# Values of the dilated head groups: which order of tokens the products read, and who regroups them

## The chip, the cores and the metric

The program runs on 1 core of one Trainium2 chip. The metric is the device time of one execution in microseconds (us), from the runs' own clock. The core has a matrix engine (TensorE: PE for the products, PEld for the loads of their stationary operand, the weights of a matmul), VectorE (DVE), ScalarE (ACT), GpSimd (POOL), and SyncE (SP), which only issues DMAs here. Each engine works through its own instructions in the order in which they are written. Two memories lie on the core: SBUF, 128 partitions wide, and PSUM, into which TensorE writes.

## The reference

A stack of transformer blocks over 512 tokens with a width of 1024, in float32. The change lies in the first two layers, whose mixer A is a dilated sliding-window attention in three groups of four heads. Group 0 reads neighbouring tokens; for group 1 (dilation 4) and group 2 (dilation 16) the tokens are regrouped first, so that every fourth (or sixteenth) token comes together:

```python
DSW_GROUPS = ((128, 1), (512, 4), (2048, 16))

def to_sub(a):
    a = a.reshape(B, L, dilation, H, hd).transpose(0, 2, 3, 1, 4)
    return jnp.pad(a, ((0, 0), (0, 0), (0, 0), (0, Lp - L), (0, 0)))
...
h = rmsnorm(x, norm1[l])
proj = h @ w_in[l]
qa, ka, va, qb, kb, vb, gate_pre = jnp.split(proj, splits, axis=-1)
...
p = jnp.exp(scores - mx)
den = jnp.sum(p, axis=-1, keepdims=True)
o = jnp.einsum('brhnqk,brhnkc->brhnqc', p, vw) / den
```

The values `va` of one group are 512 tokens by 256 columns (4 heads of 64). A second mixer B (`qb`, `kb`, `vb`), gates, an output product and a feed-forward part follow; further blocks after the second layer are not touched.

## The kernel before

**Products.** Every float32 operand is held as two float32r parts, `hi` and `lo`. `mm3` (L215 to L219) makes one product from three matmuls: hi*hi (L217), hi*lo (L218), lo*hi (L219). The weights of the model come as chunks of up to 1024 rows by 256 columns. `unit` (L495) takes 128 columns of a chunk as the stationary operand and streams the 512 tokens of x past them, 24 matmuls of 512 columns. `unit_tok` (L503) does it the other way: the stationary operand is 128 tokens of x (`xh[k][:, toks]`, a 128x128 block), and the chunk's 256 columns are streamed, again 24 matmuls (8 pieces of the width, three each). The result has tokens on partitions. One such unit of 128 tokens is called a tile here.

**Values.** `v_chunk` (L569) makes the values of one group in four tiles. With `perm`, which holds for `v1` and `v2`, tile j takes the tokens j, j+4, j+8, ...: `dsl(j, P, 4)` picks every fourth column of `xh` and `xl`, so that the regrouping happens in the read of the stationary operand. `vb` and `v0` take 128 neighbouring tokens, `slice(j * P, (j + 1) * P)`. ACT then moves the tile out of PSUM, scaled by the norm's factor of each token (L580), into `va[g]`, where each pair of heads has a block of ones between its two blocks of 64. The factors in regrouped order are columns 4 to 7 of `rcol`, made by four small DMAs from POOL in `norm_gen` (L473).

**Order.** Nothing is scheduled by a planner; the order of the Python code is the order on each engine. After each unit `tick` (L192) emits: pieces of the split of the next chunk (`pump`, L125: hi by ACT at L111, lo by DVE at L112) and, where a chunk is through, the load of the chunk three further on (L89, on SP's queue); then the evacuation of the unit; then one step of every background generator. The generators around the change are `mixer_b` (L652), whose last step is eight matmuls at L724 after the first tile of `v1`; `mixer_a_exp` (L761), which regroups the scores' maxima by DMAs from POOL (L770, L778) and then subtracts (DVE, L786) and takes exp (ACT, L787), one job a tick; and `mixer_a` (L795), which begins with the chunks `ga` after `v2`: transposes of the scores (L834), copies of them (L837), and, a tick later, the products with the values `va` (L819), in the order group 1, 2, 0.

**Buffers.** Tiles of 128x512 made by `t` (L62) share 45 buffers, those of PSUM share 8, raw chunks have 3. A new user of a buffer waits until the former one's last reader is done.

Of the kernel before, what the change touches and what calls it, by code (L numbers as in the profile page):

```python
# [4 lines left out]
F32 = mybir.dt.float32  # L5
# [6 lines left out]
P = 128  # L12
# [7 lines left out]
# columns of the packed parameters, each vector as columns of 128  # L20
# [11 lines left out]
# columns of the packed constants  # L32
# [8 lines left out]
class Ctx:  # L41
    """Pools, the weight stream and the clock that interleaves background work with dense units."""
# [82 lines left out]
    def pump(self, npieces=None):  # L125
        """Emit pieces of the split of the chunk after the one in use, and the loads behind it.

        Without a number: so many that the split is through a unit before the chunk in use is."""
        if npieces is None:
            left, self.ticks = self.ticks, max(1, self.ticks - 1)  # L130
            if not self.todo and self.nsplit < min(len(self.chunks), self.cur + self.ahead):
                self._start_split()
            npieces = -(-len(self.todo) // max(1, left - 1))
        self._pieces(npieces)
        while self.loaded < min(len(self.chunks), self.nsplit - (1 if self.todo else 0) + 3):
            self._load()
# [15 lines left out]
    def next(self, name, ticks=2):  # L152
        """(hi, lo) of the next chunk of the plan."""
        i = self.cur
        assert self.chunks[i]["name"] == name, (self.chunks[i]["name"], name)
        self.hl.pop(i - 2, None)
        self.ahead = 1
        while self.nsplit <= i or (self.nsplit == i + 1 and self.todo):
            self.pump(1)
        self.cur = i + 1  # L160
        self.ticks = ticks
        return self.hl.pop(i)

# [38 lines left out]
    def settle(self):  # L202
        """Emit what was put off to the next tick."""
        later, self.later = self.later, []
        for f in later:
            f()
# [14 lines left out]
    def split(self, src, name, scale=None):  # L221
        """hi and lo parts of src (times a column of scales)."""
        nc = self.nc
        h = self.t(name + "h", F32R)
        l = self.t(name + "l", F32R)
        n = src.shape[-1]
        hv, lv = h[:, 0:n], l[:, 0:n]
        if scale is None:
            nc.scalar.activation(hv, src, AF.Copy)
            nc.vector.tensor_tensor(lv, src, hv.bitcast(F32), op=SUB)  # L230
        else:
            nc.scalar.activation(hv, src, AF.Copy, scale=scale)
            nc.vector.scalar_tensor_tensor(lv, src, scale, hv.bitcast(F32), op0=MUL, op1=SUB)
        return hv, lv


class Parts:
    """Rows k, 256 columns each, two to a tile."""
# [24 lines left out]
def make_plan(a):  # L263
# [15 lines left out]
    # the first chunk comes in parts, to start early  # L279
# [51 lines left out]
    # the last products go through twice  # L331
# [19 lines left out]
class Kern(Ctx):  # L351
# [45 lines left out]
    def norm_begin(self, gain, gain2=None):  # L397
        """gain: fn(j) -> column of x's factor. gain2: fn(j), factor whose squares are also summed."""
        self.norm_ready = False
        self.ngain, self.ngain2 = gain, gain2  # L400
        self.xh, self.xl = [None] * KT, [None] * KT
        self.sqs = [[], []]

    def sumsq(self, src, slot, scale=None, apart=False, to=0, dve=False):
        """Add src's squares to one of the slot's list of sums, or start another."""
        nc = self.nc
        n = src.shape[-1]
        acc = self.sqs[slot]
        q = self.t("sq")[:, 0:n]
        if scale is None:  # L410
            nc.scalar.activation(q, src, AF.Square)  # L411
        else:
            nc.scalar.activation(q, src, AF.Square, scale=scale)
        if not acc or apart:
            acc.append(q)
        else:
            (nc.vector if dve else nc.gpsimd).tensor_tensor(acc[to], acc[to], q, op=ADD)  # L417

    def norm_tile(self, j):
        """Split of x[j] for the next products, and its squares."""  # L420
        g = self.ngain(j)
        self.xh[j], self.xl[j] = self.split(self.x[j], "x", scale=g)
        dve = j == KT - 1
        self.sumsq(self.x[j], 0, dve=dve)
        if self.ngain2 is not None:
            self.sumsq(self.x[j], 1, scale=self.ngain2(j), dve=dve)

    def rsqrt(self, v, n, out=None):
        """v^-0.5 of an SBUF tile [P, n]."""
        nc = self.nc  # L430
# [12 lines left out]
    def colsum(self, sq, nt, dim):  # L443
        """[P, nt] of mean + eps of the summed squares, tokens on partitions."""
# [11 lines left out]
    def rows(self, r, nt):  # L456
        """PSUM [P, nt*P]: r's columns as rows, the same on every partition."""
        ps = self.ps()
        for T in range(nt):
            self.nc.tensor.matmul(ps[:, T * P:(T + 1) * P], lhsT=r[:, T:T + 1].to_broadcast([P, P]), rhs=self.ident, start=True, stop=True)  # L460
        return ps[:, 0:nt * P]

    def norm_gen(self, perm=False, rows=True):
# [4 lines left out]
        rcol = self.pc.tile([P, 8], F32, tag="rcol", bufs=2, name=self.nm("rcol"))  # L468
        r = self.rsqrt(v, 4, None if two else rcol[:, 0:4])
        if perm:  # L470
            # every fourth token
            for T in range(4):
                nc.gpsimd.dma_start(rcol[32 * T:32 * T + 32, 4:8], rcol[:, T:T + 1])  # L473
        yield
        if two:
# [3 lines left out]
            # u = mean((x g)^2) + eps; wanted: r^2 mean + eps  # L479
# [15 lines left out]
    def unit(self, ps, hl, nt, ks, first=True, last=True, xs=None, k0=0):  # L495
        """Features nt*128.. of a chunk, transposed: out [features, tokens]."""
# [6 lines left out]
    def unit_tok(self, ps, hl, toks, xs=None, rhs=None):  # L503
        """Tokens of a chunk's all columns: out [tokens, columns]."""
# [8 lines left out]
    def late_pair(self, hl, early, late, xs=None, mid=None):  # L513
        """Two units at once: the operands of the late k come last."""
# [12 lines left out]
    def first_pair(self, hl, ev, gen):  # L527
        """The first two units after a norm: the last tiles of x come late."""
        p = self.late_pair(hl, range(0, 6), (6, 7), mid=gen)
        self.tick(lambda: ev(0, p[0]), lambda: ev(1, p[1]))  # L530
# [14 lines left out]
    def mixer1(self, l):  # L545
        nc = self.nc
        # per two heads: values, ones, values
# [21 lines left out]
        def v_chunk(name, dst, perm):  # L569
            hl = self.next(name, 4)  # L570
            for j in range(4):
                p = self.ps()
                self.unit_tok(p[:, 0:256], hl, dsl(j, P, 4) if perm else slice(j * P, (j + 1) * P))

                def ev(p=p, j=j):
                    o, i = dst[:, j], p[:, 0:256]
                    if dst is not vb:
                        o, i = o[:, :, dsl(0, 2, 2)], i.rearrange("p (a b c) -> p a b c", a=2, b=2)
                    c = 4 + j if perm else j
                    nc.scalar.activation(o, i, AF.Copy, scale=self.rcol[:, c:c + 1])  # L580
                self.tick(ev)

        if l == 0:
            # x comes in tile by tile
# [3 lines left out]
            self.first_pair(self.next("kb"), ev_q(kT, "b", None, False), self.norm_gen(perm=True))  # L588
        else:
            self.first_pair(self.next("qb"), ev_q(qT, "b", 0.125, False), self.norm_gen(perm=True))  # L590
# [22 lines left out]
        def ev_g(dst):  # L613
            # sigmoid(y) = (1 + tanh(y / 2)) / 2; kept: tanh
# [37 lines left out]
    def mixer_b(self, qT, kT, vb, oB):  # L652
# [3 lines left out]
        for hp in range(2):  # L656
            po = None
            for hh in range(2):
# [30 lines left out]
                # wide parts go in two passes  # L689
# [38 lines left out]
    def mixer_a_scores(self, g, qT, kT, st):  # L728
# [3 lines left out]
        # heads of one bank share their rows of the PE array  # L732
# [28 lines left out]
    def mixer_a_exp(self, st):  # L761
        """exp of the scores less the maximum over all groups."""
        nc = self.nc
        m = st["m"]
        # the maximum, in both orders of the tokens
# [145 lines left out]
    def mem_norm(self):  # L911
        """mem's mean squares: rows and columns of the factors."""
# [40 lines left out]
    def mem_k(self):  # L953
        """K^T [head dim, 256 tokens] of each head of the memory."""
# [10 lines left out]
    def mem_v(self, done=None):  # L965
        """V [tokens, heads * dim] of the memory."""
# [12 lines left out]
    def even(self):  # L979
# [50 lines left out]
        for i in range(2):  # L1030
# [26 lines left out]
            if i == 0:  # L1057
                # the norm between the blocks scales x itself
# [11 lines left out]
    def out_proj(self, name, cat, ks=range(8), late=2):  # L1070
        """x += the transposed product of the tiles cat with the next chunks; the last of ks come late."""
# [17 lines left out]
    def xattn(self, l):  # L1089
# [8 lines left out]
        def halves(v):  # L1098
            """The two parts of 256 columns in one tile."""
# [6 lines left out]
        def scores(h):  # L1106
            # softmax(r s): the queries' factors r are not yet in s
# [85 lines left out]
    def rope_table(self):  # L1193
        """Rows 64-95 cos, 96-127 the signed sin of the positions' angles, 0-63 ones."""
# [12 lines left out]
        # 2 pi in parts of few bits  # L1207
# [4 lines left out]
        # rows of cos: sin(pi/2 - |r|)  # L1212
# [10 lines left out]
    def odd(self):  # L1223
# [68 lines left out]
        # up-projections of the latents  # L1292
# [33 lines left out]
        # the matrix memory  # L1326
# [4 lines left out]
        # 2 sigmoid(y) = 1 + tanh(y / 2)  # L1331
# [34 lines left out]
        # the last heads come beside the first products  # L1366
# [46 lines left out]
    def mla(self, qT, kT, mv, ha):  # L1413
        nc = self.nc
        # queries' tile T: keys 0..(T+1)*128
# [76 lines left out]
    def mlstm_gates(self, gt, out):  # L1492
# [33 lines left out]
        # beside twice the sums  # L1526
# [11 lines left out]
    def mlstm(self, qm, km, vm, g4, so, hm, nv):  # L1538
# [24 lines left out]
        def s2(h):  # L1563
# [21 lines left out]
            # the last two heads' means side by side  # L1585
# [40 lines left out]
    def down_final(self, ah, al):  # L1626
        """The last products and the last norm, in halves of the tokens."""
# [176 lines left out]
```

## Time and profile before

| | |
|---|---|
| median of 3 runs | 2814.88 us (2813.25 to 2814.93) |
| profiled execution, span from first to last instruction | 2811.2 us |
| median less that span | 3.7 us |
| PE busy, DVE, ACT, POOL (share of the span) | 99%, 53%, 37%, 12% |
| mean granted TensorE clock | 0.996 |

The profile is of one execution, and its span leaves out what lies around the first and the last instruction; no time of its own beside the span is given for it, so the span and the median of the runs stand 3.7 us apart for whatever reasons. Busy shares are means over the whole span. Matmuls overlap: a row's duration is longer than the distance from its start to the next one's, and the distance is what a tile costs.

### The profile page before, as it was taken

How to read it: one execution, taken by the hardware profiler on the slowest of the kernel's cores; microseconds unless marked ns; L12 is line 12 of the kernel's file. 1: busy time of each engine (PE TensorE's matmuls, PEld its weight loads, DVE VectorE, ACT ScalarE, POOL GpSimd, SP SyncE). 2: the span in 40 equal slices, each digit the busy share in tenths (PEclk: the TensorE clock that was granted, in tenths of full speed). 3: DMA queues.
4: the chain of work that ended last, by engine and by line, in shares of the span. 5: the costliest groups of instructions: out<-in, count | busy, mean ns of one | idle time of the engine just before them, and what ended most of it. 6: DMA issues, size and time to landing. Idle time of an engine off the chain costs nothing.

```text
span 2811.2 us, 33273 instructions
## 1 busy us (share of the span) xinstructions
PE 2780.3 (99%) x13358; PEld 2320.8 (83%) x13358; DVE 1483.8 (53%) x2533; ACT 1046.7 (37%) x1967; POOL 340.2 (12%) x402
## 2 busy tenths in 40 slices
PE   9999999999999999999999999999999999999998
PEld 7798888888878988788888887888888788788887
DVE  5533765445554356645466666434356646643434
ACT  5333343333343434423243354322243535532223
POOL 2110110001111002201021111000011001110002
PEclk9999999999999999999999999999999999999999
DMA  5112323322321114223223323232232112333321
GB/s 186 60 48 66 98 90 105 102 94 79 109 82 46 60 61 135 90 90 104 92 89 109 105 83 116 91 104 90 94 88 86 46 54 82 105 97 98 100 88 53
DMA packets 245306, 251.42 MB, mean 89 GB/s; under 512 B 7424, under 2 KB 243200, under 8 KB 244640
## 3 DMA queue, kind: packets, MB, share of 16 engines
q1 hardware_dynamic: 242592, 243.58, 27.0%
q0 software_dynamic: 1552, 4.93, 0.5%
q8 instruction: 104, 1.70, 0.3%
q10 hardware_dynamic: 1008, 0.80, 0.1%
q14 instruction: 50, 0.41, 0.1%
HBM read 247.15 MB, written 2.10 MB: 89 GB/s over the span
## 4 chain that ended last, share of the span: by engine, by line
PE 93%; DVE 3%; ACT 2%; issue 1%; POOL 0%; DMA 0%; POOLq 0%; ACTq 0%; DVEq 0%
PE ps L217 29%; PE ps L218 28%; PE ps L219 28%; DVE lo L112 1%; PE ps L819 1%; PE ps L747 1%; PE ps L1476 1%; PE ps L724 1%; PE ps L667 1%; PE ps L1427 1%; DVE x L540 0%; PE ps L1151 0%; PE ps L834 0%; PE ps L451 0%; PE ps L460 0%
## 5 line engine op out<-in xcount | busy, mean ns | idle before, releaser
L217 PE MATMUL ps<-xh,hi 128*128 128x512 f32 x2224 | 875.1, 393 | 5.1 <-ACT hi L111 5.1
L219 PE MATMUL ps<-xh,lo 128*128 128x512 f32 x2224 | 868.9, 391 | 1.4 <-DVE lo L112 1.4
L218 PE MATMUL ps<-xl,hi 128*128 128x512 f32 x2224 | 868.5, 391 | 0.0
L112 DVE TENSOR_TENSOR lo<-raw,hi 128x512 fp32r<-128x512 f32 (+2 forms) x922 | 636.1, 747 | 197.2 <-ACT hi L111 196.0
L111 ACT ACTIVATE hi<-raw 128x512 fp32r<-128x512 f32 (+2 forms) x922 | 506.6, 617 | 324.7 <-PE ps L218 255.2
L217 PEld LDWEIGHTS ps<-xh,hi 128*128 128x128 f32 x2224 | 419.0, 188 | 93.4 <-ACT hi L111 5.7
L219 PEld LDWEIGHTS ps<-xh,lo 128*128 128x128 f32 x2224 | 418.9, 188 | 91.0 <-DVE lo L112 3.1
L218 PEld LDWEIGHTS ps<-xl,hi 128*128 128x128 f32 x2224 | 419.0, 188 | 84.9 <-issue 0.2
L218 PE MATMUL ps<-actl,hi 128*128 128x512 f32 (+1 forms) x752 | 282.7, 376 | 0.3 <-DVE actl L230 0.3
L217 PE MATMUL ps<-acth,hi 128*128 128x512 f32 (+1 forms) x752 | 282.8, 376 | 0.0
L219 PE MATMUL ps<-acth,lo 128*128 128x512 f32 (+1 forms) x752 | 282.6, 376 | 0.0
L540 DVE TENSOR_TENSOR x<-ps,x 128x512 f32<-128x512 f32 x136 | 93.5, 688 | 266.6 <-PE ps L219 266.6
L218 PEld LDWEIGHTS ps<-actl,hi 128*128 128x128 f32 x752 | 141.6, 188 | 26.0 <-DVE actl L230 0.5
L219 PEld LDWEIGHTS ps<-acth,lo 128*128 128x128 f32 x752 | 141.6, 188 | 25.6
L217 PEld LDWEIGHTS ps<-acth,hi 128*128 128x128 f32 x752 | 141.6, 188 | 25.5
L861 DVE TENSOR_TENSOR a<-ps,Rb 128x512 f32<-128x512 f32 x88 | 60.6, 691 | 182.4 <-PE ps L219 174.8
L417 POOL TENSOR_TENSOR sq<-sq,sq 128x512 f32<-128x512 f32 (+1 forms) x73 | 94.6, 1300 | 436.4 <-ACT sq L411 431.2
L872 POOL TENSOR_TENSOR y<-y,Rb 128x512 f32<-128x512 f32 x44 | 57.3, 1302 | 589.3 <-ACT y L868 589.3
L217 PE MATMUL ps<-hi,xh 128*128 128x256 f32 x384 | 128.3, 334 | 0.0
L872 POOL TENSOR_TENSOR a<-a,Rb 128x512 f32<-128x512 f32 x44 | 58.2, 1326 | 571.0 <-ACT a L871 571.0
L218 PE MATMUL ps<-lo,xh 128*128 128x256 f32 x384 | 123.4, 321 | 0.0
L219 PE MATMUL ps<-hi,xl 128*128 128x256 f32 x384 | 123.4, 321 | 0.0
(367 smaller groups left out, 3178.0 us busy)
## 6 DMA issues: line engine op xcount, KB each, us to landing
raw<-in_w_up SPq DMA_DIRECT2D x44, 1024.0 KB, 5.1
raw<-in_ffn_w_gate_up SPq DMA_DIRECT2D x44, 1024.0 KB, 5.1
raw<-in_w_in SPq DMA_DIRECT2D x39, 1024.0 KB, 5.1
raw<-in_w_down SPq DMA_DIRECT2D x16, 1024.0 KB, 5.1
raw<-in_ffn_w_down SPq DMA_DIRECT2D x16, 1024.0 KB, 5.1
raw<-in_od_w_in SPq DMA_DIRECT2D x10, 1024.0 KB, 5.3
raw<-in_w_o SPq DMA_DIRECT2D x8, 1024.0 KB, 5.1
raw<-in_xattn_wkv SPq DMA_DIRECT2D x8, 1024.0 KB, 5.2
```

Source lines behind the costliest of these rows:

```text
L111: nc.scalar.activation(g(hi, d), g(raw, s), AF.Copy)
L112: nc.vector.tensor_tensor(g(lo, d), g(raw, s), g(hi, d).bitcast(F32), op=SUB)
L217: mm(out, lhsT=wh, rhs=xh, start=first, stop=False)
L218: mm(out, lhsT=wh, rhs=xl, start=False, stop=False)
L219: mm(out, lhsT=wl, rhs=xh, start=False, stop=last)
L417: (nc.vector if dve else nc.gpsimd).tensor_tensor(acc[to], acc[to], q, op=ADD)
L540: self.nc.vector.tensor_tensor(self.x[j], ps, self.x[j], op=ADD)
L667: nc.tensor.matmul(z[b][:, o:o + n], lhsT=k[rs, kt * P:(kt + 1) * P], rhs=q[rs, kt * P:S], start=(kt != 3), stop=False, skip_group_check=True)
L724: nc.tensor.matmul(po[rs, kt * P:S], lhsT=vb[:, kt, h * 64:(h + 1) * 64], rhs=ag[kt], start=(kt == 0), stop=(kt == 3))
L747: nc.tensor.matmul(ps[:, c:c + P], lhsT=qT[(g, hp)][rs, T * P:(T + 1) * P], rhs=kT[(g, hp)][rs, (T - prev) * P:(T - prev + 1) * P], start= ...
L861: nc.vector.tensor_tensor(t, ps, self.Rb, op=MUL)
L872: nc.gpsimd.tensor_tensor(t, t, self.Rb, op=MUL)
```

## The change

`v_chunk` no longer picks every fourth token. All four tiles of `v1` and `v2` take 128 neighbouring tokens, as `vb` and `v0` do, with the natural-order factors `rcol[:, j]`. ACT writes the scaled tile into a temporary tile `vn` (128x256, from the 45 shared buffers), and four DMAs on SP's queue, one for each head, spread it: the 128 partitions of `vn` go to 32 partitions times 4 token groups of `va`, in pieces of 64 float32 (256 bytes), 32 KB a DMA. That is 16 DMAs a chunk and 64 in the two layers. The regrouped factors and their eight POOL DMAs are gone. The rest of the diff takes comments out.

```diff
-    def norm_gen(self, perm=False, rows=True):
+    def norm_gen(self, rows=True):
...
-        rcol = self.pc.tile([P, 8], F32, tag="rcol", bufs=2, name=self.nm("rcol"))
+        rcol = self.pc.tile([P, 4], F32, tag="rcol", bufs=2, name=self.nm("rcol"))
         r = self.rsqrt(v, 4, None if two else rcol[:, 0:4])
-        if perm:
...
-            for T in range(4):
-                nc.gpsimd.dma_start(rcol[32 * T:32 * T + 32, 4:8], rcol[:, T:T + 1])
...
-                self.unit_tok(p[:, 0:256], hl, dsl(j, P, 4) if perm else slice(j * P, (j + 1) * P))
+                self.unit_tok(p[:, 0:256], hl, slice(j * P, (j + 1) * P))
 
                 def ev(p=p, j=j):
-                    o, i = dst[:, j], p[:, 0:256]
+                    i = p[:, 0:256]
+                    r = self.rcol[:, j:j + 1]
+                    if perm:
+
+                        t = self.t("vn")[:, 0:256]
+                        nc.scalar.activation(t, i, AF.Copy, scale=r)
+                        v = t.rearrange("p (a b c) -> p a b c", a=2, b=2)
+                        for a in range(2):
+                            for b in range(2):
+                                nc.sync.dma_start(dst[32 * j:32 * j + 32, :, a, 2 * b], v[:, a, b])
+                        return
+                    o = dst[:, j]
                     if dst is not vb:
                         o, i = o[:, :, dsl(0, 2, 2)], i.rearrange("p (a b c) -> p a b c", a=2, b=2)
-                    c = 4 + j if perm else j
-                    nc.scalar.activation(o, i, AF.Copy, scale=self.rcol[:, c:c + 1])
+                    nc.scalar.activation(o, i, AF.Copy, scale=r)
                 self.tick(ev)
```

On SP's queue at `v1` and `v2` of the first layer stood only loads of weight chunks before (`raw`):

```order
L89 DMA raw_1133<-in_w_in 128x8x256
L89 DMA raw_1365<-in_w_in 128x8x256
L89 DMA raw_1538<-in_w_in 128x8x256
L89 DMA raw_1672<-in_w_in 128x8x256
L89 DMA raw_1744<-in_w_in 128x8x256
L89 DMA raw_1858<-in_w_in 128x8x256
```

Now the regrouping DMAs stand between them, four for each tile (`va_192` are the values of group 1, `va_193` of group 2):

```order
L89 DMA raw_1129<-in_w_in 128x8x256
L89 DMA raw_1361<-in_w_in 128x8x256
L581 DMA va_192<-vn_1461 32x4x64 x4
L581 DMA va_192<-vn_1511 32x4x64 x4
L89 DMA raw_1544<-in_w_in 128x8x256
L581 DMA va_192<-vn_1546 32x4x64 x4
L581 DMA va_192<-vn_1583 32x4x64 x4
L581 DMA va_193<-vn_1624 32x4x64 x4
L581 DMA va_193<-vn_1661 32x4x64 x4
L89 DMA raw_1698<-in_w_in 128x8x256
L581 DMA va_193<-vn_1700 32x4x64 x4
L581 DMA va_193<-vn_1735 32x4x64 x4
```

One load now has 8 of these DMAs ahead of it, the next 16 more, and the one after those the last 8. On PE, at the first products of mixer A with the values, in the second unit's tick of `ga`, stood before (transposes of the scores, then the products; the names in brackets are what is waited for):

```order
L834 MATMUL ps_1808<-cst,S_1325 128x128 [waits PE_49,Activation_49]
L834 MATMUL ps_1808<-cst,S_1334 128x128 [waits Activation_49]
L834 MATMUL ps_1808<-cst,S_1325 128x128
L834 MATMUL ps_1808<-cst,S_1334 128x128
L819 MATMUL ps_1753<-pt_1760,va_192 128x128 [waits Activation_49]
L819 MATMUL ps_1754<-pt_1760,va_192 128x128 [waits PE_49]
```

Now the same instructions stand there, and the first two products wait for the DMAs on SP's queue too (`DMAHW`):

```order
L840 MATMUL ps_1844<-cst,S_1321 128x128 [waits Activation_49]
L840 MATMUL ps_1844<-cst,S_1330 128x128 [waits Activation_49]
L840 MATMUL ps_1844<-cst,S_1321 128x128
L840 MATMUL ps_1844<-cst,S_1330 128x128
L825 MATMUL ps_1789<-pt_1796,va_192 128x128 [waits DMAHW6_49,DMAHW3_49,DMAHW7_49,DMAHW2_49,Activation_49]
L825 MATMUL ps_1790<-pt_1796,va_192 128x128 [waits DMAHW4_49,DMAHW0_49]
```

The order on PE, DVE and ACT is otherwise the same, instruction by instruction; on POOL the eight DMAs of `rcol` are gone.

## Rows read from the trace of the kernel before

**Rows 1.** Page: busy time of each engine, and the closing chain by engine.

```profile
PE 2780.3 (99%) x13358; PEld 2320.8 (83%) x13358; DVE 1483.8 (53%) x2533; ACT 1046.7 (37%) x1967; POOL 340.2 (12%) x402
PE 93%; DVE 3%; ACT 2%; issue 1%; POOL 0%; DMA 0%; POOLq 0%; ACTq 0%; DVEq 0%
```

**Rows 2.** Groups by form, v0 (134.5 to 154 us): busy us, mean ns | idle before.

```profile
L218 PE MATMUL ps<-lo,xh 128*128 128x256 f32 x32 | 9.1, 283 | 0.0
...
L218 PEld LDWEIGHTS ps<-lo,xh 128*128 128x128 f32 x32 | 6.1, 191 | 0.0
```

**Rows 3.** Groups by form, v1 and v2 (165 to 205 us), same columns.

```profile
L218 PE MATMUL ps<-lo,xh 128*128 128x256 f32 x56 | 22.3, 399 | 0.0
...
L218 PEld LDWEIGHTS ps<-lo,xh 128*128 128x128 f32 x55 | 18.3, 333 | 0.0
```

**Rows 4.** Timeline of ACT, value tiles, exp, pieces: start, us, instruction, [idle before].

```profile
151.19 0.48 ACT L580 ACTIVATE va<-ps,rcol 128x256 f32<-128x256 f32 x1 [3.72 <-PE ps L219]
...
154.06 0.47 ACT L580 ACTIVATE va<-ps,rcol 128x256 f32<-128x256 f32 x1 [0.45 <-PE ps L219]
...
176.02 0.47 ACT L580 ACTIVATE va<-ps,rcol 128x256 f32<-128x256 f32 x1 [4.69 <-PE ps L219]
...
182.07 1.14 ACT L787 ACTIVATE S<-S 128x512 f32<-128x512 f32 x2
183.11 1.14 ACT L111 ACTIVATE hi<-raw 128x512 fp32r<-128x512 f32 x2
...
193.06 0.47 ACT L580 ACTIVATE va<-ps,rcol 128x256 f32<-128x256 f32 x1 [3.65 <-PE ps L219]
...
204.42 0.47 ACT L580 ACTIVATE va<-ps,rcol 128x256 f32<-128x256 f32 x1 [4.17 <-PE ps L219]
```

**Rows 5.** Windows: us, busy of PE, PEld, DVE, ACT, POOL, granted clock, DMA.

```profile
134.70:156.20 21.50, 21.36 (x160) 18.45 (x159) 11.96 (x24) 11.51 (x26) 3.83 (x13) 1.00 0.15 49
156.20:204.20 48.00, 48.00 (x203) 46.59 (x202) 12.32 (x22) 12.97 (x26) 5.23 (x12) 1.00 0.14 45
...
888.10:936.10 48.00, 48.00 (x204) 46.59 (x203) 12.33 (x22) 13.01 (x26) 5.28 (x12) 1.00 0.15 45
```

**Rows 6.** Timeline of PE: mixer B's last step, and the first products with values.

```profile
162.05 2.37 PE L724 MATMUL ps<-at,vb 128*64 128x512 f32 x8
164.35 0.51 PE L217 MATMUL ps<-hi,xh 128*128 128x256 f32 x1
...
216.93 1.95 PE L819 MATMUL ps<-pt,va 128*128 128x128 f32 x16
...
225.05 1.95 PE L819 MATMUL ps<-pt,va 128*128 128x128 f32 x16
```

**Rows 7.** Timeline of DVE: the last split piece in v2, and those in ga.

```profile
195.12 0.69 DVE L112 TENSOR_TENSOR lo<-raw,hi 128x512 fp32r<-128x512 f32 x1 [3.79 <-ACT hi L111]
...
220.34 2.50 DVE L112 TENSOR_TENSOR lo<-raw,hi 128x512 fp32r<-128x512 f32 x4 [2.19 <-ACT hi L111]
```

**Rows 8.** DMAs: one line's issues (ns min/median/max), and issues with median us to landing.

```profile
L89 SPq DMA_DIRECT2D raw<-in_w_in x39: 367/368/858, 7.4 to 984.8; - x39
...
raw<-in_w_in SPq DMA_DIRECT2D x39, 1024.0 KB, 5.1
...
out_dram<-o SPq DMA_DIRECT2D x10, 128.0 KB, 1.8
...
rcol<-rcol POOLq DMA_DIRECT2D x8, 0.5 KB, 2.7
mp<-m POOLq DMA_DIRECT2D x8, 2.0 KB, 1.6
```

**Rows 9.** What reads or writes rcol: ns min/median/max, first and last start.

```profile
L473 POOL DMA_DIRECT2D rcol<-rcol x8: 548/552/607, 29.5 to 752.2; - x8
L580 ACT ACTIVATE vb<-ps,rcol x8: 473/474/477, 33.5 to 774.1; 128x256 f32<-128x256 f32 x8
```

**Rows 10.** Timeline of POOL in v1: the DMAs of mixer A's maxima.

```profile
166.15 2.19 POOL L770 DMA_DIRECT2D mp<-m  x4 [8.59 <-DVE mq L772]
```

More of the change, by code (lines that the diff above doesn't have):

```diff
@@ L587, in mixer1 @@
             self.tick(lambda: ev(0, p[0]), lambda: ev(1, p[1]))
-            self.first_pair(self.next("kb"), ev_q(kT, "b", None, False), self.norm_gen(perm=True))
+            self.first_pair(self.next("kb"), ev_q(kT, "b", None, False), self.norm_gen())
         else:
-            self.first_pair(self.next("qb"), ev_q(qT, "b", 0.125, False), self.norm_gen(perm=True))
+            self.first_pair(self.next("qb"), ev_q(qT, "b", 0.125, False), self.norm_gen())
             self.pair("kb", ev_q(kT, "b", None, False))
```

## The prediction

> **What bounds the kernel now.** I read the page first: PE is busy 99% of the span and makes 93% of the chain that ended last [rows 1]. So a microsecond taken off PE's own work is a microsecond off the end, as long as what feeds PE keeps ahead. The question is then what a value tile costs PE, read or not read in steps of four. The groups by form answer it in part: in `v0`, with neighbouring tokens, a 128x256 matmul lasts 283 ns and its weight load 191 ns [rows 2]; in `v1` and `v2`, the same instruction with the same shapes, 399 and 333 ns [rows 3]. Only the step of the read differs. Since matmuls overlap, these durations are not the cost of one; the cost is the distance between tiles. ACT's timeline gives it, because each evacuation waits for the last matmul of its tile (the releaser in the brackets). Where PE has only value tiles between two evacuations, it is 154.06 - 151.19 = 2.87 us in `v0`, and (204.42 - 176.02) / 5 = 5.68 us in `v1` and `v2` [rows 4], which is 0.120 and 0.237 us for each of the 24 matmuls. [...]
>
> **The change, part by part.**
>
> *PE's tiles.* Two chunks of four tiles in two layers are 16 tiles, each brought from 5.68 to 2.87 us: 16 x 2.81 = 45.0 us less. A second way to it: `v1` and `v2` take 48.00 us in either layer [rows 5], of which mixer B's last eight matmuls are 164.35 - 162.05 = 2.30 [rows 6]; the other 45.70 become 8 x 2.87 = 22.96 and some 0.3 for the two places where PE changes from one kind of work to another, so 22.4 a layer and 44.9 in all. Both ways agree; I take 45.0.
>
> [...]
>
> *ACT's evacuation.* It writes one contiguous tile instead of four blocks with gaps. The blocks took 0.47 us and the contiguous `vb` 474 ns [rows 4, 9]: no change.
>
> *POOL.* Eight DMAs of 0.55 us go [rows 9]. POOL is busy 12% and has no share in the chain [rows 1]: worth nothing.
>
> *SP's queue.* 64 DMAs of 32 KB come. The trace has none of their kind. Issuing one takes SP 0.37 us for a 1 MB load [rows 8]; four are 1.5 us for a tile of 2.87. From issue to landing the nearest rows are 1.6 us (`mp`, the same spread of 128 partitions to 32 by 4, in smaller pieces) and 1.8 us (`out_dram`, from SP), the far ones 2.7 (`rcol`) and 5.1 (1 MB) [rows 8]. I take 1.8. A DMA also waits on this queue until the one eight before it has landed; eight are two tiles, 5.7 us, above even the 5.1. So SP keeps pace with PE.
>
> Who waits for them: PE at the first products with the values. These start at 216.93 (group 1) and 225.05 (group 2), the last evacuation of `v2` at 204.42 [rows 4, 6]; these 12.5 and 20.6 us are `ga`'s own units, transposes and products and do not shrink. Group 1's last tile is ready another 4 x 2.87 = 11.5 us earlier, so 24 us ahead. A landing of 2 or of 5 us is hidden; the cover is gone only when DMAs run 20 us late. The buffers of `vn` are taken again by copies and gates in `ga` at the earliest one unit after `v2`, more than 5 us: nothing either.
>
> What is queued behind them on SP: the loads of later chunks. The load behind the first eight is of the chunk three after `v2`. It goes out in the third tile of `v1`, some 17 us before `v2`'s end (six tiles), and its split runs first about 15 us after that end (DVE at 220.34 [rows 7]). With 5.1 us to land [rows 8] some 27 us are left; the next load has as much. Cost nothing.
>
> *The shorter cover.* ACT's 13.0 and DVE's 12.3 us of work in `v1` and `v2` now have some 25.6 us (48.0 - 22.4) instead of 48. `v0` is the nearest row: 11.51 and 11.96 us of work in 21.50, and PE still busy 21.36 [rows 5], a loss of 0.14. The tightest point is the split of `ga`'s first chunk, which PE needs right after `v2`. Its last piece ends at 195.12 + 0.69 = 195.81 [rows 7], 2.75 us after the evacuation of `v2`'s second tile at 193.06 [rows 4]. Two tiles follow that evacuation, 5.74 us in the new kernel, so 3.0 us are left; the split before `v2` stands the same way in `v1`, where ACT has fewer exp. I take no cost; if this margin were lost and two tiles more, PE would wait 2.7 us at each of four such places, 11 us in all, which is the other end.
>
> *The maxima of mixer A.* Their DMAs issue from 166.15, 1.8 us after mixer B's last matmuls give way at 164.35 [rows 6, 10]; the fourth starts some 1.6 later and lands after 1.6 [rows 8], so 5.05 after it. With shorter tiles DVE asks for them (L775) behind a tile, its evacuation and a split piece on ACT and on DVE, about 2.87 + 0.47 + 0.6 + 0.69 = 4.6 us after it [rows 4, 7] and may wait 0.5 us. Behind it stand the first subtractions, whose exp comes on ACT only after `v1`'s last tile, 4 us later. Nothing reaches PE.
>
> The sum: 2811.2 - 45.0 = 2766.2 us of span; with the 3.7 us between that span and the median, 2769.9, so **2770 us**.
>
> **The rivals.**
>
> *Feeding falls short.* The order of work on ACT and DVE is made for long tiles, and the splits come late at chunk ends. For it: in the first tick of `v2` ACT has 0.47 + 1.14 + 1.14 = 2.75 us to do in a tile of 2.87 [rows 4]. Against: one tick only, and `v0` above. Price 11 us: 2781.
>
> [...]
>
> *SP's queue gives it back, and more: slower.* The place is the queue from `v1`'s first tile to group 2's first product. If its small DMAs don't overlap but run one after the other, 32 a layer at t us each must fit into 23 us of tiles plus the 20.6 us of `ga`, 43.6; each further microsecond is PE's wait. The saving of 22.4 a layer is eaten from 32 t = 66, t = 2.06 us. With 2.7 us (`rcol` [rows 8]) it would be 86.4, PE waits 42.8 a layer, and 2 x (42.8 - 22.4) = 41 us are lost: 2856. Against: the four `mp` DMAs issue within 2.19 us [rows 10] and land 1.6 each, so they overlap; and 1 MB lands in 5.1 us [rows 8], where one DMA here has 32 KB. [...]
>
> **How the numbers follow.** The forecast gets 0.88: price and count both come from rows of the same instruction, twice over. Feeding falls short 0.07, the pace stays 0.02, SP's queue 0.03. The predicted time is the likeliest case's, 2770. Its own spread is small: the runs of before lie 1.7 us apart, the two ways to the sum 0.1, unseen waits of some 2 us. I let the range go from 2767 up to 2779, most of the way to the feeding case; the rest of that, the unchanged pace and the queue are left out, about 0.1 together with what may lie below. A difference of 0.2% is about what a measurement of this kernel can tell from none. Faster: 0.88 + 0.07 = 0.95; same 0.02; slower 0.03.
>
> **What would show it.** The step by PE: in `v1` and `v2` matmuls near 283 ns and weight loads near 191, evacuations 2.87 us apart, and the stretch some 25.6 us instead of 48.0 in both layers. SP: regrouping DMAs landing in 1.6 to 5 us, loads as before at 5.1. No wait of PE for a DMA at the products with values, and none for ACT or DVE pieces at the start of `v2` and of `ga`. Wrong would be: tiles that stay at 5.68; idle PE before the first product with values, with SP's DMAs as releaser; idle PE before the first unit of `ga`; or a granted clock below 1.00 in these stretches.

## The result, and the profile after

| | before | after |
|---|---|---|
| median of the runs | 2814.9 us (2813.25 to 2815.63) | 2771.4 us (2769.2 to 2772.8) |
| ratio, 95% interval | | 0.9845 [0.9833, 0.9857] |
| span of the profiled execution | 2811.2 us | 2769.7 us |
| from v0's first evacuation to v2's last, first layer | 137.87 to 204.42: 66.55 us | 140.22 to 184.48: 44.26 us |
| the same, second layer | 869.79 to 936.36: 66.57 us | 849.80 to 894.06: 44.26 us |

The changed kernel is 43.5 us faster, against the 45 forecast. The stretch that was changed became 22.3 us shorter in each layer, 44.6 us together. The page after, busy time and closing chain (before: [rows 1]):

```profile
PE 2736.8 (99%) x13358; PEld 2276.2 (82%) x13358; DVE 1485.2 (54%) x2533; ACT 1047.6 (38%) x1967; POOL 335.6 (12%) x394
PE 94%; DVE 3%; ACT 2%; issue 1%; POOL 0%; DMA 0%; POOLq 0%; ACTq 0%; DVEq 0%
```

PE lost 43.5 us of busy time and PEld 44.6; nothing else moved by more than 5 us, and the chain still runs on PE. The groups by form in `v1` and `v2` (165 to 184 us) answer [rows 3]; columns: busy us, mean ns | idle before:

```profile
L218 PE MATMUL ps<-lo,xh 128*128 128x256 f32 x54 | 15.3, 283 | 0.0
...
L218 PEld LDWEIGHTS ps<-lo,xh 128*128 128x128 f32 x53 | 10.2, 192 | 0.0
```

The same instruction on the same shapes now has the durations of `v0` [rows 2]. ACT's timeline after, the last value tile of `v0` and the last six of `v1` and `v2` (before: [rows 4]); columns: start, us, instruction, [idle before, releaser]:

```profile
156.42 0.47 ACT L586 ACTIVATE va<-ps,rcol 128x256 f32<-128x256 f32 x1 [0.45 <-PE ps L219]
...
170.02 0.48 ACT L577 ACTIVATE vn<-ps,rcol 128x256 f32<-128x256 f32 x1 [1.89 <-PE ps L219]
172.90 0.47 ACT L577 ACTIVATE vn<-ps,rcol 128x256 f32<-128x256 f32 x1 [2.40 <-PE ps L219]
...
175.78 0.47 ACT L577 ACTIVATE vn<-ps,rcol 128x256 f32<-128x256 f32 x1 [0.33 <-PE ps L219]
...
178.66 0.47 ACT L577 ACTIVATE vn<-ps,rcol 128x256 f32<-128x256 f32 x1
...
181.67 0.46 ACT L577 ACTIVATE vn<-ps,rcol 128x256 f32<-128x256 f32 x1
...
184.48 0.47 ACT L577 ACTIVATE vn<-ps,rcol 128x256 f32<-128x256 f32 x1
```

The last five tiles are 2.89 us apart in the mean, (184.48 - 170.02) / 5, instead of 5.68. Read the brackets from the top down: ACT waits for PE at the first four, and from 178.66 on there is no idle time left before an evacuation. ACT has become tight there, but PE has not: in the window of after that holds `v1` and `v2` (before: [rows 5], same columns) PE is busy throughout, at a granted clock of 1.00.

```profile
158.40:184.50 26.10, 26.10 (x207) 24.64 (x206) 12.01 (x22) 13.59 (x27) 5.42 (x12) 1.00 0.32 79
```

SP's timeline after, from `v1` on. The loads (L89) stand between the regrouping DMAs (L581), as the order showed:

```profile
162.27 7.86 SPq L581 DMA_DIRECT2D va<-vn  x8
170.22 0.54 SPq L89 DMA_DIRECT2D raw<-in_w_in  x1
170.86 11.49 SPq L581 DMA_DIRECT2D va<-vn  x16
182.52 0.47 SPq L89 DMA_DIRECT2D raw<-in_w_in  x1
183.08 5.82 SPq L581 DMA_DIRECT2D va<-vn  x8
```

The 16 in the middle take 11.49 us, 0.72 each, so four of them 2.87 us: as long as a tile. Not all of that is issuing: the first four of them take 2.5 us (170.86 to 173.4), and in the rest SP also waits for tiles that ACT has not yet written and for the landing of a load (the eighth DMA behind each of the first two loads waits 0.5 us for it; in the second layer two such waits take 1.6 us). So SP has little slack in this stretch, and its last regrouping DMA goes out by 188.90, 4 us after the last evacuation is through (184.95). The line's own view after gives issue times (ns min/median/max) and landings:

```profile
L581 SPq DMA_DIRECT2D va<-vn x64: 547/593/1248, 162.3 to 897.7; - x64
...
who waited for it (us, times):
...
DMA to landing us min/median/max: 1.8/2.5/6.1
```

Nothing stands behind "who waited for it". PE's timeline after shows the places where it might have waited, the first unit of `ga` and the first products of groups 1 and 2 (before: [rows 6]); none has a bracket, so none had idle time before it:

```profile
184.22 0.40 PE L217 MATMUL ps<-xh,hi 128*128 128x512 f32 x1
...
196.90 1.95 PE L825 MATMUL ps<-pt,va 128*128 128x128 f32 x16
...
205.02 1.95 PE L825 MATMUL ps<-pt,va 128*128 128x128 f32 x16
```

DVE's timeline after has the two rows on which the shorter cover could be read: the wait for the maxima, and the last split piece of `ga`'s first chunk (before: [rows 7]):

```profile
169.19 0.17 DVE L781 TENSOR_TENSOR mq<-mq,mp 128x16 f32<-128x16 f32 x1 [0.34 <-DMA mp<-m]
...
181.80 0.69 DVE L112 TENSOR_TENSOR lo<-raw,hi 128x512 fp32r<-128x512 f32 x1 [1.22 <-ACT hi L111]
```

**What is missing.** 44.6 us went out of the two stretches, but the spans differ by 41.5. The table shows where most of the rest went: the first evacuation of `v0` comes 2.35 us later, before any changed product has run. The rest, 0.8, lies in the 1,875 us behind the second layer's `v2`; that tail differs by up to 1.7 us among the profiles of these kernels, and I did not follow it. The 2.35 us arise at about 28 us, where DVE works out the norm's factor. Start of after, timeline of DVE and POOL:

```profile
27.90 1.91 DVE L432 TENSOR_SCALAR ri<-v 128x4 int32<-128x4 int32 x1
...
28.31 1.48 POOL L546 MEMSET va<- 128x512 f32 x3
```

The same in before:

```profile
27.09 0.17 DVE L432 TENSOR_SCALAR ri<-v 128x4 int32<-128x4 int32 x1
...
28.07 1.48 POOL L550 MEMSET va<- 128x512 f32 x3
```

An operation on 128x4 numbers takes 0.17 us in one and 1.91 in the other, where it ends with POOL's memsets of the value buffers. In the profiled execution of before, DVE reached it 0.8 us earlier and was past it; so some 0.8 of the 2.35 us is that DVE came later, and most of the rest the longer operation. PE needs the result: the copy of the factor (`Rb`) starts at 30.67 in before and 33.03 in after.

### The profile page after: what moved, and what is told of

It reads as the page before. It is cut to its first block, busy times and chain, and to the rows that moved or that the text cites. A ratio compares the mean times of both kernels' runs of the same rounds, so it can differ in the third digit from the quotient of the medians.

```text
span 2769.7 us, 33431 instructions
## 1 busy us (share of the span) xinstructions
PE 2736.8 (99%) x13358; PEld 2276.2 (82%) x13358; DVE 1485.2 (54%) x2533; ACT 1047.6 (38%) x1967; POOL 335.6 (12%) x394
## 4 chain that ended last, share of the span: by engine, by line
PE 94%; DVE 3%; ACT 2%; issue 1%; POOL 0%; DMA 0%; POOLq 0%; ACTq 0%; DVEq 0%
PE ps L217 29%; PE ps L219 28%; PE ps L218 28%; DVE lo L112 1%; PE ps L825 1%; PE ps L753 1%; PE ps L1482 1%; PE ps L730 1%; PE ps L673 1%; PE ps L1433 1%; PE ps L451 0%; PE ps L1157 0%; PE ps L840 0%; DVE x L536 0%; PE ps L460 0%
## 5 line engine op out<-in xcount | busy, mean ns | idle before, releaser
L217 PE MATMUL ps<-hi,xh 128*128 128x256 f32 x384 | 113.4, 295 | 0.0
L218 PE MATMUL ps<-lo,xh 128*128 128x256 f32 x384 | 108.6, 283 | 0.0
L219 PE MATMUL ps<-hi,xl 128*128 128x256 f32 x384 | 108.5, 283 | 0.0
```

Of the source, the lines that this page charges most:

```text
L217: mm(out, lhsT=wh, rhs=xh, start=first, stop=False)
L218: mm(out, lhsT=wh, rhs=xl, start=False, stop=False)
L219: mm(out, lhsT=wl, rhs=xh, start=False, stop=last)
```

## The experiments

The medians of before beside these runs were 2814.8 to 2814.9 us; ratios are to the runs of before on the same chip.

**The changed kernel again**, beside the experiments.

> The changed kernel once more, to stand beside the others of this call. Expected 2771 us. A second question is its start: in its first profile the copy of Rb starts at 33.03 us instead of 30.67, a DVE instruction of 0.17 us (the shift at L432) having taken 1.91 us while POOL set the blocks of ones. If that comes from the change, this profile has it again; if it is the chance of when x lands, it may be gone, and the span is then 2767 to 2768.

2770.96 us (2770.79 to 2771.24), ratio 0.9847 [0.9832, 0.9861]. The stretch from `v0` to `v2` is 44.26 us again, and DVE's operation at 27.68 lasts 1.90.

**DMAs without the natural order**: the products read every fourth token again, and the result goes through `vn` and 64 DMAs all the same. The tiles come out in regrouped order here, so each DMA goes from 128 partitions to the same 128, and not to 32 by 4.

```diff
--- before
+                    if perm:
+                        t = self.t("vn")[:, 0:256]
+                        nc.scalar.activation(t, i, AF.Copy, scale=self.rcol[:, 4 + j:5 + j])
+                        v = t.rearrange("p (a b c) -> p a b c", a=2, b=2)
+                        for a in range(2):
+                            for b in range(2):
+                                nc.sync.dma_start(dst[:, j, a, 2 * b], v[:, a, b])
+                        return
```

> Only the order of the tokens is undone: v1 and v2 again read every fourth token as stationary operand, with the regrouped factors, but their tiles still go through vn and 64 DMAs of 32 KB on SP's queue. Theory (the step of the read is what cost 45 us, the DMAs are hidden): tiles of 5.68 us, weight loads of 333 ns, the time of the kernel before, 2815 +- 3 us. Rival (part of the gain came from the other edits: the contiguous evacuation, the DMAs on POOL that are gone, the splitting of work between queues): clearly below 2812, down to 2771.

2815.44 us (2813.61 to 2817.59), ratio 1.0004 [0.9993, 1.0014]: no gain. The groups by form in `v1` and `v2` of this kernel:

```profile
L218 PEld LDWEIGHTS ps<-lo,xh 128*128 128x128 f32 x55 | 18.3, 333 | 0.0
```

The weight load is back at 333 ns to the digit [rows 3], and the stretch at 66.61 us a layer. The eight POOL DMAs of the factors are still in this kernel; the run on steps below, where they are gone, tells them from the read.

**The natural order without the DMAs**: ACT writes the tile straight into `va`; the regrouping is left out.

```diff
--- after
-                    if perm:
+                    if False:
```

> The regrouping is left out: v1 and v2 read 128 neighbouring tokens and ACT writes the tile straight into va, no vn and no DMAs on SP, so the values of groups 1 and 2 are paired with the wrong tokens. It measures what the 64 DMAs cost on the path. Theory (hidden): the same as the changed kernel within 1 us, 2770 to 2772. Rival (SP's queue, 0.6 us an issue instead of the 0.37 assumed, or contention with the loads of chunks, costs something): faster by 2 us or more.

2770.30 us (2769.09 to 2772.07), ratio 0.9843 [0.9826, 0.9859]. Against 2770.96 with the DMAs, 64 DMAs cost 0.7 us, less than the 3.0 us over which the runs without them lie. So the two halves are apart: the read makes the whole gain, and the regrouping costs nothing that can be told from none.

**How the load's time goes with the step**: `v1` reads every second token, `v2` every third, so the values are other ones.

```diff
--- after
-                self.unit_tok(p[:, 0:256], hl, slice(j * P, (j + 1) * P))
+                self.unit_tok(p[:, 0:256], hl, dsl(256 * (j // 2) + j % 2, P, 2) if name == "v1" else
+                              dsl(j, P, 3) if name == "v2" else slice(j * P, (j + 1) * P))
```

> The changed kernel with other tokens as stationary operand: in v1 every second token, in v2 every third, so the values of groups 1 and 2 come from wrong tokens; all else is as in the changed kernel. It asks what about the step costs. [...] Rival A (any step but 1 costs the same): 333 ns and 5.68 us in both, 2815 us in all. Rival B (the cost grows with the bytes that are spanned): 238 ns for step 2, 286 ns for step 3.

2779.61 us in one run. Groups by form, `v1` with step 2 (158 to 170.5 us):

```profile
L218 PEld LDWEIGHTS ps<-lo,xh 128*128 128x128 f32 x28 | 5.5, 198 | 0.0
```

and `v2` with step 3 (173 to 188 us):

```profile
L218 PEld LDWEIGHTS ps<-lo,xh 128*128 128x128 f32 x27 | 7.1, 263 | 0.0
```

So 191, 198, 263 and 333 ns at steps 1, 2, 3 and 4. A cost that any step brings (rival A, 333 for all) falls, and so does one that grows evenly from step 1 on (rival B, 238 and 286). The distances between tiles say it more sharply. ACT's timeline in this kernel, the last two tiles of `v1`, then the first and the last of `v2`:

```profile
167.50 0.48 ACT L578 ACTIVATE vn<-ps,rcol 128x256 f32<-128x256 f32 x1 [1.89 <-PE ps L219]
170.37 0.48 ACT L578 ACTIVATE vn<-ps,rcol 128x256 f32<-128x256 f32 x1 [2.40 <-PE ps L219]
...
174.53 0.47 ACT L578 ACTIVATE vn<-ps,rcol 128x256 f32<-128x256 f32 x1 [1.61 <-PE ps L219]
...
187.31 0.47 ACT L578 ACTIVATE vn<-ps,rcol 128x256 f32<-128x256 f32 x1 [2.75 <-PE ps L219]
```

A tile takes 2.87 us at step 2, as at step 1, and (187.31 - 174.53) / 3 = 4.26 at step 3, which is three quarters of the 5.68 at step 4. Half of 5.68, 2.84, lies just under what a tile takes without gaps. So from step 2 to 4 the cost grows with the length of memory that the 128 columns span (65 and 70 ns a load for one more step), above a floor that steps 1 and 2 share. POOL's DMAs are gone in both chunks, and the load still follows the step. The number of columns alone, 128 each time, does not give its time. What in the longer span costs the time these four steps do not show: anything that grows in the same proportion would fit. Whether the cost goes on growing beyond step 4 is open too; a step of eight could tell, and no run has it.

**Where the cover of the DMAs ends**: each regrouping DMA cut into two, then into four (128 and 256 in the two layers in place of 64).

```diff
--- after
-                                nc.sync.dma_start(dst[32 * j:32 * j + 32, :, a, 2 * b], v[:, a, b])
+                                for c in range(0, 64, 32):
+                                    nc.sync.dma_start(dst[32 * j:32 * j + 32, :, a, 2 * b, c:c + 32], v[:, a, b, c:c + 32])
```

(with 16 in place of 32 for the four)

> Each regrouping DMA of the changed kernel is cut into two of 32 columns, 64 a layer instead of 32; the result is the same. SP takes about 0.66 us from one to the next of them in the changed kernel, so 64 take 42 us from 162 us on, to 204 us, and land by 207; group 2's first product stands at 205. Theory (the cover is 20 us of the products' other work, and issue on SP is what uses it up): PE waits 0 to 3 us a layer, 2771 to 2777. Rival (each DMA holds the queue until it has landed, 2.5 us): the 64 take 160 us, PE waits over 100 us a layer, 2990.

2769.38 us in one run: still hardly anything. SP's timeline in this kernel, and PE's waits for the values in it:

```profile
171.05 22.10 SPq L582 DMA_DIRECT2D va<-vn  x32
193.25 0.55 SPq L89 DMA_DIRECT2D raw<-in_w_in  x1
193.89 11.31 SPq L582 DMA_DIRECT2D va<-vn  x16
```

```profile
PE ps L826 <- DMA va<-vn: 2.0, 3, 0.8
```

SP is not done before 205.2 and PE begins to wait, 2.0 us over the two layers together: this is the edge. The rival, by which each DMA holds the queue until it has landed, falls. I expected 2 to 8 us more; some 2 of these lie outside the experiment, since in this execution DVE was not held up at the start (`Rb` at 30.61).

> Each regrouping DMA is cut into four of 16 columns, 128 a layer; the result is the same. Theory as for the cut into two: 128 x 0.66 = 84 us from 162 us on, to 247 us and 249 with the landing, while group 2's first product would stand at 205; PE waits 40 to 45 us a layer there or for the late loads of chunks behind these DMAs, 2850 to 2865 us, slower than the kernel before. Rival (the DMAs stay hidden, since what counts is bytes, which are the same): 2771.

2852.29 us in one run. SP's timeline, PE's first product of group 2, and PE's waits from 150 to 300 us:

```profile
162.27 21.66 SPq L582 DMA_DIRECT2D va<-vn  x32
...
184.69 42.75 SPq L582 DMA_DIRECT2D va<-vn  x64
...
228.18 21.00 SPq L582 DMA_DIRECT2D va<-vn  x32
```

```profile
242.76 0.77 PE L826 MATMUL ps<-pt,va 128*128 128x128 f32 x2 [29.72 <-DMA va<-vn]
```

```profile
PE ps L826 <- DMA va<-vn: 36.1, 4, 29.7
```

128 DMAs of 0.68 us are 86.9 us a layer (162.27 to 249.18). PE waits 36.1 us for them in the first layer and 69.2 in the run, out of the 81 that were lost against the changed kernel. Behind the waits PE works at a lower clock (granted 0.75 from 203 to 213 us, 0.57 from 242.7 to 250, where the changed kernel has 1.00 at the same products), which takes a part of the other 12 (14 products with group 2 take 3.33 us there, where all 16 take 1.95 in the changed kernel); how much in all was not worked out. So the slower rival of the prediction has the place and the sum right: it names 86.4 us of queue a layer for its 2856. Its condition does not hold: the DMAs do overlap on their way (median 1.8 us from issue to landing, with one issued every 0.68), and what goes one after the other is their issue. At 0.6 to 0.7 us each, the kernel's 32 a layer (some 23 us) stay far below the 66 us at which the saving would be eaten.

**Another queue**: the regrouping DMAs issued from ACT.

```diff
--- after
-                                nc.sync.dma_start(dst[32 * j:32 * j + 32, :, a, 2 * b], v[:, a, b])
+                                nc.scalar.dma_start(dst[32 * j:32 * j + 32, :, a, 2 * b], v[:, a, b])
```

> The regrouping DMAs are issued from ACT's queue instead of SP's; the result is the same. Issuing is then ACT's own time, in order with its work: four of 0.6 us are 2.4 us a tile, on top of 0.5 to 2.75 us of work, in a tile of 2.87. Theory (feeding is the next bound behind the tiles, with 2 to 3 us of margin for the splits): ACT falls behind by 1 to 2 us in each of v2's tiles, the split of ga's first chunk is late, PE waits at v2's end in both layers, 3 to 8 us in all, 2774 to 2779. Rival (margins are wide): 2771.

2786.04 us (2785.34 to 2786.19), ratio 0.9897 [0.9881, 0.9914]: 15 us more than with SP's queue, twice what I expected at most. ACT's timeline in this kernel:

```profile
185.85 1.15 ACT L793 ACTIVATE S<-S 128x512 f32<-128x512 f32 x2 [2.59 <-DMA va<-vn]
186.91 0.61 ACT L111 ACTIVATE hi<-raw 128x512 fp32r<-128x512 f32 x1
187.43 0.45 ACT L577 ACTIVATE vn<-ps,rcol 128x256 f32<-128x256 f32 x1
187.91 2.51 ACTq L581 DMA_DIRECT2D va<-vn  x4
190.47 1.16 ACT L793 ACTIVATE S<-S 128x512 f32<-128x512 f32 x2 [2.59 <-DVE S L792]
191.53 0.45 ACT L577 ACTIVATE vn<-ps,rcol 128x256 f32<-128x256 f32 x1
```

Four issues take 2.5 us of ACT in each tile. With them a tile costs ACT over 4 us and PE 2.88, and the last evacuation of `v2` comes at 191.53 in place of 184.26 in the changed kernel run again. I expected the loss at the split of `ga`'s first chunk; PE waits there no more than 1.0 us. PE's timeline shows the place:

```profile
201.77 3.78 PE L825 MATMUL ps<-pt,va 128*128 128x128 f32 x16 [5.04 <-ACT pt L843]
```

The backlog is carried through `ga`'s first unit to the copies of the transposed scores. It costs 5 to 6 us a layer there, and then as much as 1.8 more, as the 16 products take 3.78 us in place of 1.95. From 201.8 to 205.5 the granted clock is 0.50, against 1.00 at the same products in the changed kernel, after a stretch in which PE was busy 0.23 of 5.20 us. So ACT has no room for eight times 2.5 us in this stretch; SP, which has only loads to issue, has.

**The start**: the memsets of the value buffers moved behind the first value chunk in the program.

```diff
--- after
-        for g in range(3):
-            nc.gpsimd.memset(va[g][:, :, :, 1], 1.0)
...
         v_chunk("vb", vb, False)
+        for g in range(3):
+            nc.gpsimd.memset(va[g][:, :, :, 1], 1.0)
```

> The changed kernel with POOL's blocks of ones for va set after vb's chunk instead of at the head of the layer. Theory (POOL's three memsets hold up a DVE instruction of the first norm, which PE then waits for): the shift at L432 takes 0.2 us, PE does not wait for rcol at 31 us, 1.5 to 2 us faster than the changed kernel, 2769. Rival (the late start is the chance of when x lands): same as the changed kernel.

2770.17 us (2769.15 to 2771.39), ratio 0.9844 [0.9829, 0.9859]. In the profile the operation lasts 0.17 us, `Rb` starts at 30.86 and the span is 2767.4, against 2769.4 in the profile of the changed kernel run again. The medians differ by 0.8 us only, so both were timed once more. The next two texts speak of a rotary set-up: the operation is L432, the first step of the norm's factor.

> The changed kernel with the memsets of the value buffers moved behind the first chunk of vb, timed in five rounds. If the memsets hold up the first operation of the rotary set-up in every execution, as they did in the profiles of the changed kernel (1.90 us in place of 0.17), this is about 2 us under the changed kernel of the same call: 2769.0 against 2771.0. If the collision comes only in some executions, the difference is under 1 us.

> The changed kernel itself, timed in five rounds on the same chip as the one with late memsets: 2771 us, with the first operation of the rotary set-up at 1.9 us in its profile if the collision comes every time.

Late memsets 2769.42 us (2769.22 to 2771.25), ratio 0.9839 [0.9826, 0.9853]; the changed kernel 2771.57 us (2768.99 to 2772.11), ratio 0.9842 [0.9829, 0.9855]. Timelines of DVE and POOL with late memsets:

```profile
27.04 0.17 DVE L432 TENSOR_SCALAR ri<-v 128x4 int32<-128x4 int32 x1
...
28.04 1.48 POOL L598 MEMSET va<- 128x512 f32 x3
```

and in the changed kernel beside it:

```profile
27.92 2.09 DVE L432 TENSOR_SCALAR ri<-v 128x4 int32<-128x4 int32 x1
...
28.50 1.48 POOL L546 MEMSET va<- 128x512 f32 x3
```

Spans are 2767.5 and 2770.0. But the edit did not move the memsets in time. Later in the program, they still ran right behind POOL's issue of one DMA, at 28.04 here and at 28.79 in the first profile, where before has them at 28.07. What differs is when DVE is there: its two TENSOR_SCALAR operations on integers, L432 and L434, were over by 27.41, just ahead of that issue (27.44). The same happened, with no memset moved, in the profiles of before (over by 27.46, the issue at 27.47) and of the run with twice the DMAs (27.54 and 27.63). Where one of the two came later, it lasted until the memsets ended: L432 in three profiles of the changed kernel (1.90 to 2.09 us) and in that of the DMAs without the natural order (1.22 us), L434 in the run with four times the DMAs (2.10 us) and in the run without any:

```profile
27.16 2.12 DVE L434 TENSOR_SCALAR ry<-ri 128x4 int32<-128x4 int32 x1
```

So neither theory nor rival was put to the test, and what it would be worth to move the memsets is open. Both medians with late memsets are lower, by 0.8 and 2.1 us, but single runs of both kernels lie at either value, and nothing shows that the edit is the cause.

## Why the prediction was right

**PE's tiles** were the whole of it, as forecast: 16 tiles brought from 5.68 to 2.89 us are 44.6, as measured, against 45.0 and 44.9. Both were worked out from `v0`, and the row of `v0` was the right one: same instruction, same shapes, only the step differs. That the weight load set the pace before is read from its busy time, 46.59 of 48.00 us in `v1` and `v2` at a granted clock of 1.00 [rows 5], and from the run on steps, where the tile follows the load: 198, 263 and 333 ns a load go with 2.87, 4.26 and 5.68 us a tile.

**The sum** came out 1.5 us low, 2769.9 against 2771.4, and one step behind it was right partly by luck. I added 3.7 us for "whatever reasons" between the profiled span of before and its median. The runs of the experiments list a span beside each time, and the two differ by about 1.7 us. So some 2 us of the 3.7 were something else: the profiled execution of before was itself quicker than its median, with the undisturbed start shown above. The profiled execution of after was not, so by spans alone I was 3.5 us off (2766.2 against 2769.7): 2.35 at the start, 0.8 in the tail, 0.4 in the tiles.

**ACT's evacuation**: 0.47 us, as taken. **POOL's DMAs**: the tiles make up the whole 44.6, so nothing is left for them, as taken.

**SP's queue** was the mis-sized term. I took 0.37 us for an issue from the loads and 1.8 us to land; the medians were 0.59 and 2.5 (1.9 where no load had just gone out; medians of 4.4 and 4.0 right behind one). Four issues are 2.5 us back to back, not 1.5, and 2.87 with the waits between them, so "SP keeps pace" was true with next to nothing to spare instead of with half the tile. The wait for the DMA eight before, which I put at nothing, came to 0.5 us behind each of the first layer's two loads, as its loads took 5.2 to 5.8 us to land in this stretch, and to 1.0 us at most in the second. None of it did harm, for the reason given: the products with group 2 start at 205.02, 20.5 us after the last evacuation (20.6 before), and the last DMA goes out by 188.9 and lands 1.9 us after its issue, some 14 us ahead. The run with twice the DMAs shows how much room that was: a factor of two, no more.

**The loads behind them** cost nothing, as taken: 0.47 to 0.54 us to issue in this stretch, the first of them 14 us before `v2`'s end and not 17, and PE waited nowhere for a split that had come late.

**The shorter cover.** I put 3.0 us between the last split piece and `ga`'s first unit. It is 184.22 - 182.49 = 1.7. The step that failed is that I took the piece to end 2.75 us after `v2`'s second evacuation, as in before. With ACT out of idle time it ends 182.49 - 178.66 = 3.8 after it. The direction of the rival *feeding falls short* was therefore right, and nearly half of the margin was used up. Where ACT gets 2.5 us more to do in each tile, PE does wait, but at another place than the rival names: the copies of the transposed scores.

**The maxima**: a wait of 0.34 us on DVE against 0.5, and none on PE.

**The rivals.** *The pace stays*, by which natural tiles keep 5.68 us and the time 2815, has fallen with the result (192 ns a load, 2.89 us a tile) and with the run on steps. *SP's queue* is a real limit, touched at 64 DMAs a layer of this kind and far passed at 128; the kernel issues 32.

## What to carry to other kernels

A stationary operand of 128x128 that was read with a step of four float32 columns cost TensorE 333 ns in place of 191 [rows 2, 3], and with only 256 columns streamed for each load the load was the pace (busy 46.59 of 48.00 us [rows 5]). In such a place, read in natural order and let small DMAs regroup the result, if its reader comes late enough. Step two cost nothing here, 2.87 us a tile as at step one with 256 columns streamed for each load, so it is the step to look at, not the fact of a stride. Price such DMAs by the issuing queue (0.6 to 0.7 us each) against the time until the reader, put them on a queue with nothing else to do, and count what the shorter stretch leaves to the engines beside it.

## What the runs showed of the hardware

A DVE operation on 128x4 integers, a TENSOR_SCALAR (L432 or L434), lasted 1.22 to 2.12 us in place of 0.17 in six of ten profiles (those of before, after and the experiments except the run on steps and the one from ACT's queue), until the last of POOL's three memsets was over (29.81 and 29.79 us in after), with PE waiting behind it (1.3 us for `rcol` in after). In these six it began when POOL started on the DMA issue ahead of the memsets (27.16 and 27.18 in the run without the DMAs), or later; in the other four both such operations were over by then. Operations with two tiles of 128x4 as inputs ran beside the memsets in 0.16 to 0.17 us (before, from 28.09 on). No run moved the memsets in time, so that they are the cause is read from the traces and not tested, and by what they would hold DVE up is not shown.

SP and ACT needed 0.59 and 0.61 us (medians, in after and in the run from ACT's queue) to issue a DMA that spreads 32 KB within SBUF, where a 1 MB load took 0.37 [rows 8]. Issue hardly changed with size: halves and quarters of these DMAs still cost 0.65 to 0.71 us each in the queue, so cutting them only multiplied the time.
